# Low parts of the weights by an adding DMA, and tiles that begin on lines of 64 bytes

## The chip, the core and the metric

The kernel runs on one core of one Trainium2 chip. The metric is device microseconds of one launch. The engines are named as in the profile: PE (the tensor engine's matmuls), PEld (its weight loads), DVE (vector), ACT (scalar), POOL (gpsimd), SP (the engine that issues most DMAs); a transfer is carried out by the core's 16 DMA engines.

## The reference, cut to what matters

Two transformer-like blocks work one after the other on 512 tokens of 1024 features, in float32:

```python
def first_block(x, ...):
    for layer in range(2):
        if layer < 1: x = x + fox_mixer(rmsnorm(x, ...), w_fox_in, b_f, w_fox_out)   # 16 heads of 64
        else:         x = x + mla_mixer(rmsnorm(x, ...), w_dq, ..., w_mla_out, k, v) # 16 heads of 128 + 64
        x = x + conv_ffn(rmsnorm(x, ...), w_in, conv_w, conv_b, w_out)               # 1024 -> 2 x 2816 -> 1024
    return rmsnorm(x, final_norm)

def second_block(x, ...):
    x = x + nsa_pool_mixer(rmsnorm(x), ...)      # 8 heads, three branches, and a pooling branch
    x = x + swiglu(rmsnorm(x), ...)              # 1024 -> 2 x 2816 -> 1024
    x = x + conformer_conv(rmsnorm(x), ...)      # 1024 -> 2048, gate, 31-tap convolution, layer norm, -> 1024
    x = x + swiglu(rmsnorm(x), ...)
    return rmsnorm(x)
```

## The kernel before

Activations lie with the features on the 128 partitions and the 512 tokens along the row. A matrix product in nearly full float32 precision is made of three products in float32r, a rounded form that PE takes at full rate: each operand is a high part (rounded to float32r) and a low part (what the rounding left), and `mm3` (lines 320 to 323) adds high x high (L321), high weight x low activation (L322) and low weight x high activation (L323). A weight tile is 128 rows (partitions) by 1024 columns, 512 KB in float32: eight blocks of 128 x 128, so 24 matmuls with 512 moving columns each.

`load` (line 307) brings such a tile: a DMA issued by SP into `raw` (three buffers), a cast on ACT into `hi` (three buffers), and a subtraction on DVE into `lo` (three buffers), both in `split`, L303. It is called for all weights, 417 times. The other `split`s, of activations, stay as they are.

The stages follow each other: Fox attention, a gated FFN with a short convolution, MLA attention, the same FFN again, NSA attention, a SwiGLU FFN, the conformer, a SwiGLU FFN, the last norm. Each FFN is a loop over 44 tiles of its first matrix, with `xs` (`xsh` and `xsl`) as the moving operand, and then over eight output blocks of three loads each of its second matrix, with `hh` and `hl` as the moving operand. In the attention stages the heads run in a pipeline in which POOL scales the softmax (L522), and matmuls of projections fill PE's gaps. In the conformer the 31 taps of the convolution are shared by PE (with diagonal weights made by ACT, L1296, and DVE, L1297), DVE (L1269) and POOL (L1285, with products made by ACT, L1281).

The order of instructions on each engine is set when the program is built, by a scheduler that plays the program through with its own costs; loads get a higher priority. Each engine then runs its own list strictly in order and waits on semaphores.

Of the kernel before, what the change touches and what calls it, by code (L numbers as in the profile page):

```python
# [17 lines left out]
P = 128  # L18
T = 512
# [40 lines left out]
def _lay_out(i):  # L60
    """Only layout of the inputs, and constants of the shapes."""
# [147 lines left out]
class _Fill:  # L209
    """Tensor engine work that may stand between the steps of an attention, in order."""  # L210
# [7 lines left out]
    def push(self, name, gen, at=None, gate=None):  # L218
        """gate: (step of the heads, how many heads must be past it), for tiles that are used again."""
        self.q.insert(len(self.q) if at is None else at, (name, gen, gate))  # L220
# [22 lines left out]
    def need(self, name):  # L243
        """The task of this name, to its end."""
        for task in [t for t in self.q if t[0] == name]:
            self._all(task[1])
            self.q.remove(task)
# [7 lines left out]
def _body(ctx, tc, a, out):  # L255
# [14 lines left out]

    nvec = a["vecs"].shape[1]
    vecs = cp.tile([P, nvec], F32, name="vecs")
# [15 lines left out]
    gg = cp.tile([P, NC8], F32, name="gg")  # L288
    G.memset(ones, 1.0)
    mhalf = cp.tile([P, NQ], F32, name="mhalf")  # L290
# [9 lines left out]
    def split(hi, lo, src, scale=None):  # L300
        """hi + lo is src (times scale) to float32's precision; each is exact in float32r."""
        if scale is None:
            return S.copy(hi, src), V.tensor_sub(lo, src, bc(hi))  # L303
        return (S.activation(hi, src, AF.Copy, scale=scale),
                V.scalar_tensor_tensor(lo, src, scale, bc(hi), op0=OP.mult, op1=OP.subtract))  # L305

    def load(src, k, ahead=PRIO_DMA):
        n = src.shape[-1]
        with tc.high_priority(offset=ahead):
            raw = wp.tile([P, RAW], F32, tag="raw", name="raw", bufs=3)  # L310
            nc.sync.dma_start(raw[:, :n], src)
        with tc.high_priority(offset=min(ahead, PRIO_W)):
            hi = wp.tile([P, RAW], F32R, tag="hi", name="hi")
            lo = wp.tile([P, RAW], F32R, tag="lo", name="lo")
            split(hi[:, :n], lo[:, :n], raw[:, :n])
        return [z[:, :n].rearrange("p (k c) -> p k c", k=k) for z in (hi, lo)]
# [8 lines left out]
    def mm2(acc, w, rh, rl, first, last):  # L325
        """w: hi and lo beside each other, 64 columns each; their products are added by join()."""
        PE.matmul(acc, w, rh, start=first, stop=False)
        PE.matmul(acc, w, rl, start=False, stop=last)

    def join(hi, lo, po):  # L330
        S.copy(hi, po[:64])
        V.tensor_sub(lo, po[:64], bc(hi))
        V.tensor_add(lo, bc(lo), po[64:])
# [3 lines left out]
    def lin(acc, w, act, ks, cols, first=True, last=True, w0=0):  # L337
        """acc[cols, tokens] += sum over the chunks ks of w[k][:, cols].T @ act[k]."""
        wh, wl = w
        ah, al = act  # L340
        for n, k in enumerate(ks):
            mm3(acc, wh[:, k - w0, cols], wl[:, k - w0, cols], ah[:, k], al[:, k],
                first and n == 0, last and n == len(ks) - 1)
            yield STEP
# [8 lines left out]
    class Stats:  # L353
        """Sum over features of squares, gathered chunk by chunk."""
# [26 lines left out]
    def rsqrt(dst, src, n, eps):  # L381
        v = tp.tile([P, NQ], F32, name="var", tag="var", bufs=2)
        V.tensor_scalar(v, src, 1.0 / n, eps, op0=OP.mult, op1=OP.add)
        G.tensor_tensor(dst, v, mhalf, op=OP.pow)

    def wide(r):
        """[128 tokens, 4] -> the same for every partition, [128, 512]."""
        pr = bank("pr")
        for i in range(NQ):
            PE.transpose(pr[:, sl(i)], r[:, i : i + 1].to_broadcast([P, P]), ident)  # L390
        return pr
# [6 lines left out]
    class Norm:  # L398
        """Reciprocal root mean square of the tokens. What is made of it waits until the tensor
        engine has other work in hand: evictions that need it are put off by after()."""  # L400
# [7 lines left out]
        def step(self):  # L408
            if self.t is None:
                self.t = self.pool.tile([P, NQ], F32, name=self.name + "t", tag=self.name + "t", bufs=2)  # L410
                self.square(self.t)
            elif self.b is None:
                self.b = spread(self.t, self.pool, self.name)
                for f in self.put_off:
                    f()
                self.put_off = []
# [4 lines left out]
        def tick(self):  # L421
            """A tile of products has been queued."""
            self.left -= 1
            if self.left <= 0:
                self.step()
# [16 lines left out]
    def split_x(gname, dst=None, st=None, square_on=None):  # L442
        """x times its gain, as hi and lo."""
        dst = dst or xs
        for c in range(NC8):
            last = split(dst[0][:, c], dst[1][:, c], x[:, c], vec(gname, c))
            if st is not None:
                st.add(x[:, c], square_on)
        return last
# [9 lines left out]
    def out_proj(name, act, nk, per, blocks, b0=0, k0=0, late=False):  # L459
        """x += act @ weights; with late, the last chunk of act comes in after all others."""  # L460
# [20 lines left out]
    def stack_q(f, s, name, pool):  # L481
        """Head s of a pair: hi in its own half of the partitions, lo in the other half."""
        t = pool.tile([P, T], F32R, name=name, tag=name)
        S.copy(t[own[s]], f[own[s]])
        V.tensor_sub(t[own[1 - s]], f[own[s]], bc(t[own[s]]))
        return t

    def stack_k(f, s, ka, kl):
        """hi in both halves of ka, lo in the own half of kl."""
        S.copy(ka[own[s]], f[own[s]])  # L490
        V.tensor_copy(ka[own[1 - s]], f[own[s]])
        V.tensor_sub(kl[own[s]], f[own[s]], bc(ka[own[s]]))

    class Head:
        """Softmax attention of one head in three steps: scores, transposes, values."""
# [4 lines left out]
        def scores(self):  # L500
            pool = self.pool
            nm = pool.tile([P, NQ], F32, name="nm", tag="nm", bufs=3)
            sm = pool.tile([P, NQ], F32, name="sm", tag="sm", bufs=3)
# [10 lines left out]
            rc = pool.tile([P, NQ], F32, name="rc", tag="rc", bufs=3)  # L514
# [34 lines left out]
    def pipeline(prep, n, fill, edge):  # L549
        """Heads in a pipeline, with other work of the tensor engine between their steps."""  # L550
# [21 lines left out]
    # ------------------------------------------------------------------ Fox  # L572
    def fox():
        with ExitStack() as es:
# [27 lines left out]
            def forget():  # L602
# [4 lines left out]
                # softplus(z) with z = -logit: max(z, 0) + ln(1 + exp(-|z|))  # L607
# [83 lines left out]
    # ------------------------------------------------------------- gated FFN  # L691
# [44 lines left out]
    # ------------------------------------------------------------------ MLA  # L736
# [158 lines left out]
    # ------------------------------------------------------------------ NSA  # L895
    def nsa():
        with ExitStack() as es:
# [10 lines left out]
            ccmp = kp.tile([P, NQ * 32 + NQ], F32, name="ccmp")  # L908
# [9 lines left out]
            # two norms in a row: of x, and of what comes of it  # L918
# [8 lines left out]
            r1 = kp.tile([P, NQ], F32, name="r1")  # L927

            def square(t):
                rsqrt(r1, st1.sums(), D, EPS)  # L930
                m2 = tp.tile([P, NQ], F32, name="m2", tag="m2")
# [12 lines left out]
            with phase("n_x") as pool:  # L944
                # compressed keys and values
# [160 lines left out]
            # compressed branch  # L1106
# [82 lines left out]
    # ------------------------------------------------------------ conformer  # L1189
    def conformer():  # L1190
        with ExitStack() as es:
# [9 lines left out]
            with phase("c_x") as pool:  # L1201
# [3 lines left out]
                wdh = pool.tile([P, nw], F32R, name="wdh")  # L1205
                wdl = pool.tile([P, nw], F32, name="wdl")
# [3 lines left out]
                def conv(j, z, on, n_pe):  # L1210
                    """31 taps of chunk j: the first n_pe by the tensor engine, the rest by vector or gpsimd."""
                    y = zc[:, j]
                    if n_pe:
                        zh = pool.tile([P, T + 30], F32R, name="zh", tag="zh", bufs=2)
                        zl = pool.tile([P, T + 30], F32R, name="zl", tag="zl", bufs=2)
# [14 lines left out]
                # layer norm: sums about the mean of three chunks, and the exact shift from it  # L1230
# [88 lines left out]
                def beside(gen):  # L1319
                    """Tensor engine work, with the others' share of the convolutions beside it."""  # L1320
# [35 lines left out]
            rt = pool.tile([P, NQ], F32, name="lnt")  # L1356
            dt = pool.tile([P, NQ], F32, name="lndt")
            d2 = pool.tile([P, NQ], F32, name="lnd2")
# [30 lines left out]
    def final(gname):  # L1389
# [11 lines left out]
        rt = rp.tile([P, NQ], F32, name="rt", tag="rt", bufs=2)  # L1401
# [39 lines left out]
```

## Time and profile before

| what | value |
|---|---|
| median of 3 runs | 2606.76 us (2606.7 to 2606.8) |
| profiled execution, first to last instruction | 2603.5 us |
| the rest of a launch beside that span | about 3.3 us |
| PE busy | 2526.1 us, 97% |
| DVE busy | 1627.3 us, 63% |
| ACT busy | 1140.7 us, 44% |
| POOL busy | 464.8 us, 18% |
| DMA from HBM, mean | 84 GB/s; the one load queue takes 27.1% of 16 engines' time |

PE's busy share alone doesn't say that PE is the bound everywhere: it is a mean over stages, so the stretches below are read one by one.

### The profile page before, as it was taken

Reading aid. Unit: us, or ns where it says so; the run is one execution under the profiler, and the core shown is the slowest. Engines: PE = TensorE matmul, PEld = TensorE weight load, DVE = VectorE, ACT = ScalarE, POOL = GpSimd, SP = SyncE. Lnnn points to the kernel's source line nnn. Section 1 sums busy time; section 2 is a strip of 40 time slices with the busy share of each in tenths; the row PEclk is TensorE's granted clock in tenths of the full one; section 3 lists DMA queues with packets and bytes.
Section 4 is the critical chain, followed back from the end, with each engine's and each line's share of the span. In section 5 each row is a group of like instructions: output and inputs, shape, how many; then the busy total and the mean of one; then the engine's idle time right before and its main releaser. Section 6 shows DMA issues by size and latency. Waiting matters only on the chain. (4 is left out here: it accounts for less than half of the span.)

```text
span 2603.5 us, 31317 instructions
## 1 busy us (share of the span) xinstructions
PE 2526.1 (97%) x11903; PEld 2088.6 (80%) x11903; DVE 1627.3 (63%) x2495; ACT 1140.7 (44%) x1933; POOL 464.8 (18%) x369
## 2 busy tenths in 40 slices
PE   8999999999999999999999999999999778999998
PEld 6988888888888888888888888888887546888886
DVE  7887777625677656777436996444328996544422
ACT  4664444324566544444324684222225453333221
POOL 3452000001132212000011222000004763100001
PEclk9999999999999999999999999999999988999999
DMA  4122333333311222333333212333332101333332
GB/s 150 58 66 68 103 97 97 91 97 102 88 57 55 72 73 83 102 96 95 93 93 117 64 51 84 97 97 96 89 100 73 57 17 33 99 97 97 93 97 69
DMA packets 65447, 218.90 MB, mean 84 GB/s; under 512 B 7536, under 2 KB 8560, under 8 KB 65296
## 3 DMA queue, kind: packets, MB, share of 16 engines
q1 hardware_dynamic: 65296, 216.90, 27.1%
q8 instruction: 93, 1.52, 0.3%
q14 instruction: 58, 0.48, 0.1%
HBM read 214.70 MB, written 2.10 MB: 83 GB/s over the span
## 5 line engine op out<-in xcount | busy, mean ns | idle before, releaser
L303 ACT CAST hi<-raw 128x1024 fp32r<-128x1024 f32 (+4 forms) x417 | 420.5, 1010 | 919.5 <-PE acc L322 716.2
L323 PE MATMUL acc<-xsh,lo 128*128 128x512 f32 x1792 | 700.3, 391 | 15.7 <-DVE lo L303 15.7
L321 PE MATMUL acc<-xsh,hi 128*128 128x512 f32 x1792 | 699.6, 392 | 3.0 <-ACT xsh L303 2.9
L303 DVE TENSOR_TENSOR lo<-raw,hi 128x1024 fp32r<-128x1024 f32 (+4 forms) x417 | 499.8, 1199 | 322.8 <-ACT hi L303 317.7
L322 PE MATMUL acc<-xsl,hi 128*128 128x512 f32 x1792 | 700.5, 391 | 0.8 <-DVE xsl L305 0.8
L323 PEld LDWEIGHTS acc<-xsh,lo 128*128 128x128 f32 x1792 | 338.2, 189 | 88.9 <-DVE lo L303 18.7
L321 PEld LDWEIGHTS acc<-xsh,hi 128*128 128x128 f32 x1792 | 338.2, 189 | 73.6 <-ACT xsh L303 3.3
L322 PEld LDWEIGHTS acc<-xsl,hi 128*128 128x128 f32 x1792 | 338.0, 189 | 73.1 <-DVE xsl L305 2.1
L373 POOL TENSOR_TENSOR ssum<-ssum,sq 128x512 f32<-128x512 f32 x75 | 120.4, 1609 | 1482.3 <-ACT sq L367 1472.3
L321 PE MATMUL acc<-hh,hi 128*128 128x512 f32 x704 | 279.1, 396 | 0.0
L322 PE MATMUL acc<-hl,hi 128*128 128x512 f32 x704 | 279.1, 396 | 0.0
L323 PE MATMUL acc<-hh,lo 128*128 128x512 f32 x704 | 279.1, 396 | 0.0
L522 POOL TENSOR_SCALAR lg<-lg,rc 128x384 f32<-128x384 f32 (+3 forms) x144 | 165.8, 1167 | 384.2 <-DVE rc L515 300.6
L710 DVE TENSOR_TENSOR y<-acc,r 128x512 f32<-128x512 f32 x88 | 60.4, 691 | 219.7 <-PE acc L323 219.5
L457 DVE TENSOR_TENSOR x<-x,acc 128x512 f32<-128x512 f32 x104 | 70.6, 685 | 158.6 <-PE acc L323 158.3
L323 PEld LDWEIGHTS acc<-hh,lo 128*128 128x128 f32 x704 | 132.6, 188 | 32.3
L322 PEld LDWEIGHTS acc<-hl,hi 128*128 128x128 f32 x704 | 132.6, 188 | 32.3
L321 PEld LDWEIGHTS acc<-hh,hi 128*128 128x128 f32 x704 | 132.6, 188 | 32.3
L1285 POOL TENSOR_TENSOR zc<-zc,pr 128x496 f32<-128x496 f32 (+17 forms) x79 | 127.0, 1611 | 65.2 <-ACT pr L1281 56.7
L707 DVE SCALAR_TENSOR_TENSOR y<-u,vecs,y 128x510 f32<-128x510 f32 (+1 forms) x176 | 130.9, 748 | 3.4 <-ACT y L705 0.6
L512 ACT ACTIVATE lg<-lg,nm 128x128 f32<-128x128 f32 x192 | 107.1, 560 | 47.2 <-DVE nm L510 46.3
L303 ACT CAST hh<-y 128x512 fp32r<-128x512 f32 x88 | 54.6, 621 | 135.6 <-DVE y L714 135.6
(366 smaller groups left out, 3843.1 us busy)
## 6 DMA issues: line engine op xcount, KB each, us to landing
raw<-in_ffn_in SPq DMA_DIRECT2D x88, 512.0 KB
raw<-in_swi_in SPq DMA_DIRECT2D x88, 512.0 KB
raw<-in_ffn_out SPq DMA_DIRECT2D x32, 448.0 KB
raw<-in_swi_out SPq DMA_DIRECT2D x32, 448.0 KB
raw<-in_pw SPq DMA_DIRECT2D x24, 512.0 KB
raw<-in_fox_qk SPq DMA_DIRECT2D x16, 512.0 KB
raw<-in_ffn_out SPq DMA_DIRECT2D x16, 512.0 KB
raw<-in_uqk SPq DMA_DIRECT2D x16, 512.0 KB
```

What stands on the lines that cost most here:

```text
L303: return S.copy(hi, src), V.tensor_sub(lo, src, bc(hi))
L321: PE.matmul(acc, lh, rh, start=first, stop=False)
L322: PE.matmul(acc, lh, rl, start=False, stop=False)
L323: last_mm[0] = PE.matmul(acc, ll, rh, start=False, stop=last).ins
L373: (sum_on or G).tensor_add(self.s, self.s, sq)
L457: V.tensor_add(x[:, c], x[:, c], acc)
L512: S.activation(lg, lg, AF.Exp, bias=nm[:, i : i + 1], scale=-1.0, accum_out=sm[:, i : i + 1])
L522: (V if i in self.on_v else G).tensor_scalar(self.p[i], self.p[i], rc[:, i : i + 1], None, op0=OP.mult)
L707: V.scalar_tensor_tensor(y[:, sh:], u[:, : T - sh], vec(f"cw{l}{2 - sh}", jj), y[:, sh:], op0=OP.mult, op1=OP.add)
L710: V.tensor_mul(y, acc, norm.b)
L1285: G.tensor_add(y[:, sh:], y[:, sh:], pr[:, sh:])
```

## The change

`load` no longer uses DVE. ACT makes `hi` by a cast as before and then writes -1 times `raw`, rounded in the same way, into `lo`; POOL issues a DMA that reads the same weights a second time from HBM and adds them onto `lo`. What stands there then is weight minus rounded weight, as before. `raw` has two buffers in place of three, `lo` four in place of three. Each of the 417 loads so has one more DMA, on POOL's queue, which waits for ACT.

The second part is a helper `narrow`, which allocates a tile with its row rounded up to 16 floats, 64 bytes, and uses only the first columns. It is used for all tiles with rows of other lengths (`vecs`, the tiles of 4 columns such as `nm`, `sm`, `rc`, `var`, and some in the conformer). In the built program of before, `x`, `xs`, `raw`, `hi` and `lo` begin at multiples of 64 bytes in a partition, and `hh`, `hl`, `oh`, `ol`, `poh`, `pol`, `xkh`, `xkl`, `qlh`, `qll`, `lath`, `latl` and most operands of the heads 32 bytes past one. In the changed program every tile begins at a multiple of 64. The strings and comments that go change nothing.

```diff
+    def narrow(pool, n, dt=F32, **kw):
+
+        return pool.tile([P, -(-n // 16) * 16], dt, **kw)[:, :n]
+
     nvec = a["vecs"].shape[1]
-    vecs = cp.tile([P, nvec], F32, name="vecs")
+    vecs = narrow(cp, nvec, name="vecs")
...
-    mhalf = cp.tile([P, NQ], F32, name="mhalf")
+    mhalf = narrow(cp, NQ, name="mhalf")
...
     def load(src, k, ahead=PRIO_DMA):
         n = src.shape[-1]
         with tc.high_priority(offset=ahead):
-            raw = wp.tile([P, RAW], F32, tag="raw", name="raw", bufs=3)
+            raw = wp.tile([P, RAW], F32, tag="raw", name="raw", bufs=2)
             nc.sync.dma_start(raw[:, :n], src)
         with tc.high_priority(offset=min(ahead, PRIO_W)):
             hi = wp.tile([P, RAW], F32R, tag="hi", name="hi")
-            lo = wp.tile([P, RAW], F32R, tag="lo", name="lo")
-            split(hi[:, :n], lo[:, :n], raw[:, :n])
+            lo = wp.tile([P, RAW], F32R, tag="lo", name="lo", bufs=4)
+            S.copy(hi[:, :n], raw[:, :n])
+            S.mul(lo[:, :n], raw[:, :n], -1.0)
+
+            G.dma_start(lo[:, :n], src, accum_op=OP.add)
         return [z[:, :n].rearrange("p (k c) -> p k c", k=k) for z in (hi, lo)]
...
-            nm = pool.tile([P, NQ], F32, name="nm", tag="nm", bufs=3)
-            sm = pool.tile([P, NQ], F32, name="sm", tag="sm", bufs=3)
+            nm = narrow(pool, NQ, name="nm", tag="nm", bufs=3)
+            sm = narrow(pool, NQ, name="sm", tag="sm", bufs=3)
```

ACT's list in the first matrix of the first FFN, before. `hi` and `raw` are the weight tile's (the number tells tiles apart), `y0`, `u` and `hh` those of an output block's way to the second matrix:

```order
L303 CAST hi_3155<-raw_3153 128x1024
L713 ACTIVATE y0_2991<-y0_2991 128x512
L705 ACTIVATE y0_3069<-u_3070,vecs_70 128x512
L303 CAST hh_2864<-y0_2991 128x512
L303 CAST hi_3196<-raw_3194 128x1024
```

The same place in the changed program:

```order
L319 CAST hi_3397<-raw_3395 128x1024
L320 ACTIVATE lo_3436<-raw_3433 128x1024
L712 ACTIVATE y1_3305<-u_3306,vecs_70 128x512
L319 CAST hi_3435<-raw_3433 128x1024
L320 ACTIVATE lo_3478<-raw_3475 128x1024
```

The multiplication of a tile (`raw_3433`) stands a whole tile ahead of its cast: it is the first reader of `raw`, behind the cast of the tile before.

DVE's list in the conformer, before: taps of the convolution (`zc`) with the gate (`sg`, `z`) and the low part of one weight tile between them:

```order
L1330 TENSOR_TENSOR z_16732<-acc_16663,r_16612 128x512
L1269 SCALAR_TENSOR_TENSOR zc_16492<-z_16622,vecs_70,zc_16492 128x482
L1269 SCALAR_TENSOR_TENSOR zc_16492<-z_16622,vecs_70,zc_16492 128x483
L303 TENSOR_TENSOR lo_16802<-raw_16799,hi_16801 128x1024
L1269 SCALAR_TENSOR_TENSOR zc_16492<-z_16622,vecs_70,zc_16492 128x484
L1269 SCALAR_TENSOR_TENSOR zc_16492<-z_16622,vecs_70,zc_16492 128x485
L1269 SCALAR_TENSOR_TENSOR zc_16492<-z_16622,vecs_70,zc_16492 128x486
L1327 TENSOR_TENSOR sg_16729<-acc_16700,r_16612 128x512
```

And in the changed program:

```order
L1337 TENSOR_TENSOR z_17061<-acc_16991,r_16939 128x512
L1276 SCALAR_TENSOR_TENSOR zc_16817<-z_16949,vecs_70,zc_16817 128x482
L1276 SCALAR_TENSOR_TENSOR zc_16817<-z_16949,vecs_70,zc_16817 128x483
L1276 SCALAR_TENSOR_TENSOR zc_16817<-z_16949,vecs_70,zc_16817 128x484
L1276 SCALAR_TENSOR_TENSOR zc_16817<-z_16949,vecs_70,zc_16817 128x485
L1276 SCALAR_TENSOR_TENSOR zc_16817<-z_16949,vecs_70,zc_16817 128x486
L1334 TENSOR_TENSOR sg_17058<-acc_17029,r_16939 128x512
```

The weight tile's subtraction is gone from between the taps; the rest keeps its order.

POOL's list in the conformer, before, at its own taps (`pr` are products that ACT made):

```order
L384 TENSOR_TENSOR rt_16572<-var_16578,mhalf_79 128x4
L1285 TENSOR_TENSOR zc_16492<-zc_16492,pr_16763 128x482
L1285 TENSOR_TENSOR zc_16492<-zc_16492,pr_16768 128x483
L1285 TENSOR_TENSOR zc_16492<-zc_16492,pr_16777 128x484
L1285 TENSOR_TENSOR zc_16492<-zc_16492,pr_16786 128x485
```

And in the changed program:

```order
L322 DMA lo_17238<-in_pw1 128x1024
L1292 TENSOR_TENSOR zc_16817<-zc_16817,pr_17093 128x482
L1292 TENSOR_TENSOR zc_16817<-zc_16817,pr_17098 128x483
L1292 TENSOR_TENSOR zc_16817<-zc_16817,pr_17107 128x484
L322 DMA lo_17292<-in_pw1 128x1024
L1292 TENSOR_TENSOR zc_16817<-zc_16817,pr_17116 128x485
```

The adding DMAs of the weights of the first pointwise matrix (`in_pw1`) stand between the taps, one after every third.

## Rows read from the trace of the kernel before

**Rows 1.** The page: PE's busy time, and its tenths in 40 slices.

```profile
PE 2526.1 (97%) x11903; PEld 2088.6 (80%) x11903; DVE 1627.3 (63%) x2495; ACT 1140.7 (44%) x1933; POOL 464.8 (18%) x369
...
PE   8999999999999999999999999999999778999998
```

**Rows 2.** Stretches of 65 us: Fox, first and second FFN matrix, NSA, conformer twice.

```profile
core 0: us, PE busy (x) PEld busy (x) DVE busy (x) ACT busy (x) POOL busy (x), PEclk, DMA share, GB/s
130.00:195.00 65.00, 65.00 (x398) 58.31 (x397) 55.62 (x129) 42.51 (x103) 32.97 (x28) 1.00 0.21 66
390.00:455.00 65.00, 65.00 (x288) 53.83 (x287) 47.44 (x61) 29.08 (x37) 0.00 (x0) 1.00 0.31 98
520.00:585.00 65.00, 65.00 (x279) 52.28 (x278) 19.67 (x21) 16.75 (x20) 6.21 (x4) 1.00 0.33 95
1495.00:1560.00 65.00, 62.32 (x355) 52.33 (x355) 60.89 (x186) 57.53 (x158) 18.50 (x17) 0.97 0.19 57
2015.00:2080.00 65.00, 50.95 (x198) 39.45 (x196) 65.00 (x55) 32.48 (x48) 48.55 (x30) 0.93 0.18 57
2080.00:2145.00 65.00, 44.40 (x144) 30.14 (x144) 64.97 (x90) 36.00 (x84) 43.31 (x30) 0.84 0.05 17
```

**Rows 3.** Chain of waits, conformer: shares by line, then start, us, what.

```profile
by line: DVE zc L1269 44.8%; DVE dl L1297 19.3%; DVE lo L303 11.3%; issue 7.1%; DVE z L1331 4.8%; DVE zl L303 2.7%; DVE zc L1264 2.3%; DVE d L1237 2.0%; DVE ssum L373 2.0%; DVE z L1330 1.8%; DVE sg L1327 1.2%; DVE zc L1313 0.4%; DVE s L1254
...
1996.26 2.18 DVE lo L303
...
2034.53 1.13 DVE lo L303
```

**Rows 4.** PE's timeline, MLA: start us, us, line, operation, tiles.

```profile
649.58 0.39 PE L321 MATMUL acc<-xsh,hi 128*128 128x512 f32 x1
...
655.01 0.40 PE L321 MATMUL acc<-xkh,hi 128*128 128x512 f32 x1
...
660.38 0.40 PE L323 MATMUL acc<-xkh,lo 128*128 128x512 f32 x1
```

**Rows 5.** Groups by line and shape: count, busy us, mean ns, idle before.

```profile
L303 DVE TENSOR_TENSOR lo<-raw,hi 128x1024 fp32r<-128x1024 f32 x328 | 411.0, 1254 | 209.6 <-ACT hi L303 206.5
L303 ACT CAST hi<-raw 128x1024 fp32r<-128x1024 f32 x328 | 343.9, 1051 | 649.0 <-PE acc L322 470.0 <-issue 121.6 <-PE pq L322 18.4
...
L321 PE MATMUL acc<-hh,hi 128*128 128x512 f32 x704 | 279.1, 396 | 0.0
...
L321 PE MATMUL pq<-qlh,hi 128*128 128x512 f32 x144 | 58.3, 405 | 0.0
...
L321 PE MATMUL acc<-oh,hi 128*128 128x512 f32 x96 | 38.0, 401 | 0.2 <-DVE nm L510 0.2
...
L321 PE MATMUL acc<-poh,hi 128*128 128x512 f32 x32 | 13.1, 410 | 0.3 <-DVE ol L333 0.2
...
L321 PE MATMUL pq<-lath,hi 128*128 128x512 f32 x32 | 13.1, 408 | 0.0
```

**Rows 6.** The instructions that read tile xkh: durations, starts, forms.

```profile
L321 PE MATMUL acc<-xkh,hi x24: 395/396/478, 655.0 to 672.4; 128*128 128x512 f32 x16, 128*64 128x512 f32 x8
```

**Rows 7.** Two stretches, instructions on tile lo alone: PE, PEld, DVE.

```profile
130.00:195.00 65.00, 28.91 (x85) 16.27 (x86) 9.86 (x9) 1.00 0.21 66
1495.00:1560.00 65.00, 10.87 (x27) 5.07 (x27) 5.17 (x5) 0.97 0.19 57
```

**Rows 8.** POOL's timeline in the conformer, columns as in rows 4.

```profile
1985.68 17.15 POOL L1285 TENSOR_TENSOR zc<-zc,pr 128x482 f32<-128x482 f32 x10 [20.03 <-ACT pr L1281]
...
2035.40 4.75 POOL L1285 TENSOR_TENSOR zc<-zc,pr 128x506 f32<-128x506 f32 x3 [3.94 <-ACT pr L1281]
```

**Rows 9.** Timeline of the start, all engines.

```profile
1.18 0.42 SPq L280 DMA_DIRECT2D x<-in_xt  x1
...
4.16 0.69 DVE L369 TENSOR_TENSOR ssum<-x 128x512 f32<-128x512 f32 x1 [4.16 <-DMA x<-in_xt]
...
7.53 0.28 DVE L303 TENSOR_TENSOR lo<-raw,hi 128x128 fp32r<-128x128 f32 x1
```

More of the change, by code (lines that the diff above doesn't have):

```diff
@@ L287, in _body @@
     ones = cp.tile([P, P], F32, name="ones")
-    gg = cp.tile([P, NC8], F32, name="gg")
+    gg = narrow(cp, NC8, name="gg")
     G.memset(ones, 1.0)
-    mhalf = cp.tile([P, NQ], F32, name="mhalf")
+    mhalf = narrow(cp, NQ, name="mhalf")
     G.memset(mhalf, -0.5)
@@ L381, in rsqrt @@
     def rsqrt(dst, src, n, eps):
-        v = tp.tile([P, NQ], F32, name="var", tag="var", bufs=2)
+        v = narrow(tp, NQ, name="var", tag="var", bufs=2)
         V.tensor_scalar(v, src, 1.0 / n, eps, op0=OP.mult, op1=OP.add)
@@ L409, in step @@
             if self.t is None:
-                self.t = self.pool.tile([P, NQ], F32, name=self.name + "t", tag=self.name + "t", bufs=2)
+                self.t = narrow(self.pool, NQ, name=self.name + "t", tag=self.name + "t", bufs=2)
                 self.square(self.t)
@@ L513, in scores @@
                 self.p.append(lg)
-            rc = pool.tile([P, NQ], F32, name="rc", tag="rc", bufs=3)
+            rc = narrow(pool, NQ, name="rc", tag="rc", bufs=3)
             V.reciprocal(rc, sm)
@@ L907, in nsa @@
             gates = kp.tile([P, NQ, 24], F32, name="gates")
-            ccmp = kp.tile([P, NQ * 32 + NQ], F32, name="ccmp")
+            ccmp = narrow(kp, NQ * 32 + NQ, name="ccmp")
             nc.sync.dma_start(ccmp, a["c_cmp"])
@@ L926, in nsa @@
             norm = Norm(st1, D, rp, "r", NT_N)
-            r1 = kp.tile([P, NQ], F32, name="r1")
+            r1 = narrow(kp, NQ, name="r1")
             def square(t):
                 rsqrt(r1, st1.sums(), D, EPS)
-                m2 = tp.tile([P, NQ], F32, name="m2", tag="m2")
+                m2 = narrow(tp, NQ, name="m2", tag="m2")
                 V.tensor_mul(m2, st2.sums(), r1)
@@ L1204, in conformer @@
                 wdw = vecs[:, _VECS["w_dw"][0] : _VECS["w_dw"][0] + nw]
-                wdh = pool.tile([P, nw], F32R, name="wdh")
-                wdl = pool.tile([P, nw], F32, name="wdl")
+                wdh = narrow(pool, nw, F32R, name="wdh")
+                wdl = narrow(pool, nw, name="wdl")
                 S.copy(wdh, wdw)
@@ L1213, in conv @@
                     if n_pe:
-                        zh = pool.tile([P, T + 30], F32R, name="zh", tag="zh", bufs=2)
-                        zl = pool.tile([P, T + 30], F32R, name="zl", tag="zl", bufs=2)
+                        zh = narrow(pool, T + 30, F32R, name="zh", tag="zh", bufs=2)
+                        zl = narrow(pool, T + 30, F32R, name="zl", tag="zl", bufs=2)
                         for t in (zh, zl):
@@ L1355, in conformer @@
             pool = es.enter_context(phase("c_y"))
-            rt = pool.tile([P, NQ], F32, name="lnt")
-            dt = pool.tile([P, NQ], F32, name="lndt")
-            d2 = pool.tile([P, NQ], F32, name="lnd2")
+            rt = narrow(pool, NQ, name="lnt")
+            dt = narrow(pool, NQ, name="lndt")
+            d2 = narrow(pool, NQ, name="lnd2")
             pd = bank("pd")
@@ L1400, in final @@
             PE.matmul(pt[:, i : i + 1], sq[:, sl(i)], ones[:, 0:1], start=False, stop=True)
-        rt = rp.tile([P, NQ], F32, name="rt", tag="rt", bufs=2)
+        rt = narrow(rp, NQ, name="rt", tag="rt", bufs=2)
         rsqrt(rt, pt[:, :NQ], D, EPS)
```

## Prediction

> **What bounds the kernel now.** The page comes first [rows 1]: the tensor engine (PE) is busy in 2526.1 of the 2603.5 us of the span, and the slices show where it is not: at the start, around slices 32 to 34, and at the end. Then the table of stretches [rows 2], six pieces of 65 us from the kinds of work that matter. In the gated FFNs PE is busy in all 65.00 us at a granted clock of 1.00, while the vector engine (DVE) is busy in 47.44, the scalar engine (ACT) in 29.08, the gpsimd engine (POOL) in none, and the DMA engines in 0.31 of the time. So there the split of the weights on DVE is already hidden, and taking it away gains nothing. In the conformer the picture is turned round: DVE is busy in 65.00 and 64.97 of 65 us, PE in 50.95 and 44.40, and the granted clock is down to 0.93 and 0.84 on the mean: after PE's gaps it spends part of the time at the lower of its two levels, 1.2 instead of 2.4 GHz. Last the chain of waits of that stretch [rows 3]: from 1981 to 2168 us it runs on DVE, and 11.3% of it is `lo`, the very operation that goes.
>
> PE has a second property that matters here: its matmuls of 512 columns don't all take the same time. In the first FFN matrix 288 start in 65 us, 225.7 ns each; in the second 279, 233.0 ns each [rows 2]. PE waits for nothing in either.
>
> **The change part by part: where tiles begin.** The moving operand of the first FFN matrix (`xs`) begins at a multiple of 64 bytes, that of the second (`hh`, `hl`) 32 bytes past one. Is that the cause? The MLA stage has both operands back to back [rows 4]. Up to 655.01 us PE reads `xs`: 24 matmuls from 649.58, 226.3 ns each. From 655.01 it reads `xk`, which begins 32 bytes past: 23 steps to 660.38, 233.5 ns each, with the same kind of weight and nothing else changed. So the step is 7.2 ns there and 7.3 in the FFNs; I take 6.8, since a few of the 279 are slowed by other things. After the change every tile begins at a multiple of 64. The 512-column matmuls that now read a shifted operand are 704 + 144 + 96 + 32 + 32 [rows 5] and 24 [rows 6], in each of the three products: 1032 x 3 = 3096. That is 3096 x 6.8 ns = 21 us, all of it where PE is the bound. The score matmuls of the heads have shifted operands too; they are narrower, some 280 of 512 columns' worth by the loops of the kernel, another 2 us. Together -23 us (bounds: 0, if the cause is another, and -25).
> The Trainium skill (SBUF — State Buffer, "Specifications (TRN2)") puts SBUF's lines at 16 bytes, by which a tile 32 bytes in begins on a line as well as any other and this term would be 0. The trace speaks against it, with 226.3 beside 233.5 ns, but what it shows is a coincidence of operand and offset, so the rule is kept as a rival below.
>
> **What leaves DVE.** 417 subtractions, 328 of them of 1254 ns [rows 5]. In the FFNs and attention stages PE is busy throughout [rows 2], so they are worth nothing there. In the conformer they are worth what stands on the chain: 11.3% of 187 us, 21 us [rows 3]. One `lo` there lasts 2.18 us where POOL works beside it (at 1996.26) and 1.13 where POOL is idle (at 2034.53) [rows 3, 8]. What is late next is the rest of the same DVE work, the taps (L1269) and the diagonals (L1297), which keep the chain, so most of the 21 us should come off. But POOL, with 48.55 of 65 us busy on its own taps, now also issues a DMA every three taps there, and ACT takes the multiplications. I take -15 us (bounds: 0, and -40 if PE's clock no longer falls in the 130 us of the two stretches).
>
> **What ACT gets.** 417 multiplications by -1 of the shape of the `hi` cast, 1051 ns for 1024 columns [rows 5]; with a scalar a row of this size may take a sixth more. In an FFN stretch of 12 weight tiles (288 / 24) that is 12 x 1.05 = 12.6 us on 29.08: 41.7 of 65, hidden by PE. In Fox nine `lo` are made in the stretch and in NSA five [rows 7]: 42.51 + 9 x 1.05 = 52 us, hidden, and 57.53 + 5 x 1.05 = 62.8, barely. The order of ACT does one thing well: the multiplication of the next tile stands ahead of that tile's `hi` cast, and as `lo` has four buffers and `hi` three, both wait for the same release by PE. So the add starts some 2 us after PE has left tile t-3 and is needed when PE comes to t+1: three tiles of 5.42 us, 16.3 us, less 2.1 on ACT, leaves 14 us. A load of 256 KB at the start took 2.98 us from issue to its first reader (1.18 to 4.16, [rows 9]). Even several times that is covered. The raw load has two buffers in place of three; its slot comes free when the cast is done, about 4.4 us before ACT wants the next, and a late one stalls only ACT, which has 23 us to spare in 65.
>
> **What the DMA engines get.** This is the term that decides. 417 transfers read the weights a second time, and each also reads and writes `lo` in SBUF. The raw loads take 0.31 x 65 / 12 = 1.68 us of all 16 engines for a tile of 512 KB [rows 2]. An adding transfer is nowhere in this trace. From below it costs as much as a plain one, 1.68 us; from above, if its two reads and its write follow each other without overlap, three times that, 5.04. I take two streams, 3.36 us, because a plain load already has one read and one write in its 1.68, and only the read is added. Then a tile asks for 1.68 + 3.36 = 5.04 of 5.42 us: 93% full, but under it, with 14 us of cover for queueing. It stays hidden up to 3.74 us (5.42 - 1.68), and above that the FFNs run at the pace of the DMA engines. POOL, which issues them, is idle in the FFNs [rows 2].
> The Trainium skill (Collectives: The Full Stack, "The bandwidth ceiling: the fold count and why AG ≠ RS ≠ AR") says that a DMA that adds is slower because it reads two sources and not because of the adding, and gives a measured ratio of 1.93. As an estimate from that page the add would take 3.24 us and the tile 4.92; no row here shows an adding transfer.
>
> **The start.** The first `lo` is a subtraction of 0.28 us at 7.53 [rows 9], and PE takes it at once. Now a multiplication, an issue and a transfer of about 3 us stand there, while 3.5 MB of other loads are under way; PE has first products to do meanwhile. +4 us (bounds 0 and +8).
>
> **Sum.** -23 - 15 + 4 = -34 us on the profiled execution, 2603.5 us of span and about 3.3 around it, 2606.8 together, which is also the median of the runs. 2606.8 - 34 = 2573 us.
>
> **Rivals.**
> First, the adding transfer is too slow: the DMA engines become the bound of the FFNs. For it: the margin is only 0.38 us in 5.42 and nothing here has measured it. Against: a share of 0.31 now, and 14 us of cover. At three passes a tile takes 6.72 us, 1.30 more than PE needs. The four FFNs load 44 tiles of 512 KB each and 22 tiles' worth in the second matrix, 264 in all: 264 x 1.30 = 343 us, and the 14 us of aligned second matrices (2112 x 6.8 ns) don't show: 2573 + 14 + 343 = 2930. It decides from 3.74 us on; each 0.1 us over that costs 26 us. Chance 0.19.
> Second, ACT and POOL become what DVE was in NSA and the conformer. For it: ACT at 57.53 of 65 in NSA, POOL at 48.55 in the conformer, both in order, and POOL's issue waits for ACT's multiplication with the softmax scaling or the taps queued behind it, for which PE or the layer norm waits. Against: both have idle time in every stretch shown. If the 51 weight tiles of these two stages (27 and 24 by their loads) each put their multiplication on the path, 51 x 1.05 = 54 us, and DVE's 15 us aren't won: 2606.8 - 23 + 4 + 54 = 2642. It decides when ACT's sum in a stretch reaches the 65 us. Chance 0.09.
> Third, the change of the tiles doesn't do what it seems to: where a tile begins is not what costs 6.8 ns. Then 2606.8 - 15 + 4 = 2596. Chance 0.10.
>
> **How the numbers follow.** Forecast 0.61, the rivals 0.19, 0.09 and 0.10, and 0.01 for what I haven't thought of. The forecast's own range is 2552 to 2594 (the conformer's -40 with the full alignment, or nothing from the conformer with a late start). The whole range takes in the third and the second rival and a slightly slow add: 2548 to 2660; it leaves out most of the first rival. A change of 0.2%, 5 us, is about what a measurement of this kernel can tell from none. Faster: nearly all of the forecast and most of the third rival, 0.68. Slower: the first and second rivals and a little of the rest, 0.26. The same: 0.06.
>
> **What would show it.** In the table of stretches: second FFN matrices at 288 matmuls in 65 us as the first (alignment); the DMA share in the FFNs near 0.9 with PE still at 65 of 65 (the add at two streams), or PE below it and the share near 1 (first rival). In the chain of waits: the conformer's DVE stretch near 165 us without `lo`. In PE's waits: none for POOL's transfers but at the start. The prediction is wrong if `lo` by DMA stands among PE's longest waits.

## The result, and the profile after

The changed kernel takes 2622.4 us (2618.7 to 2626.7, four runs) beside 2606.8 (2606.7 to 2608.6) for the kernel before: 1.006 times as long, with a 95% interval of 1.0045 to 1.0074. It is slower by 0.6%, where 2573 us and a gain had been forecast. The profiled execution spans 2623.2 us beside 2603.5, so 19.7 us are to be found.

In this case the FFNs are landmarks. In both profiles the 528 recorded matmuls of every second matrix are timed from the first to the last, and the 1056 of a first matrix take 240.6 us in both wherever PE doesn't wait at its start. With each FFN's start counted back from there, the rest falls to the other stages (what PE waits for in the first tiles of an FFN is counted to the stage ahead of it). "Lines" is the first experiment below, tiles on 64-byte lines without the adding DMA:

| us, profiled execution | before | lines | after |
|---|---|---|---|
| start and Fox | 256.6 | 256.4 | 264.6 |
| second FFN matrix, each of four | 123.5 | 120.6 | 120.6 |
| MLA | 387.4 | 383.8 | 383.2 |
| NSA | 220.6 | 222.1 | 245.0 |
| conformer | 267.1 | 267.0 | 268.5 |
| last norm | 15.6 | 14.9 | 17.0 |
| span | 2603.5 | 2589.2 | 2623.2 |

Each column is one profiled execution, and the one of the changed kernel, 2625.0 us as a launch, lies 2.6 us above that kernel's median; so a difference of two or three us in one stage is not safe.

The lines bring 14.3 us. The adding DMA costs 34.0, of them 22.9 in NSA and 8.2 at the start, and in the conformer it brings nothing. Stretches of the kernel after, with columns as in [rows 2]:

```profile
130.00:195.00 65.00, 64.86 (x424) 58.74 (x423) 49.78 (x128) 48.85 (x113) 36.00 (x34) 1.00 0.50 111
390.00:455.00 65.00, 65.00 (x288) 53.81 (x288) 34.37 (x48) 39.06 (x48) 10.39 (x12) 1.00 0.87 194
520.00:585.00 65.00, 65.00 (x286) 53.33 (x285) 7.20 (x10) 29.95 (x36) 16.24 (x17) 1.00 0.92 193
...
1400.00:1430.00 30.00, 22.27 (x153) 19.12 (x152) 12.50 (x19) 21.25 (x29) 5.30 (x7) 0.85 0.88 206
1430.00:1460.00 30.00, 30.00 (x139) 25.07 (x139) 17.86 (x37) 14.77 (x27) 4.33 (x5) 0.87 0.78 184
...
1495.00:1560.00 65.00, 59.55 (x348) 50.60 (x346) 55.77 (x182) 57.76 (x162) 19.79 (x20) 0.97 0.30 71
...
0.00:20.00 20.00, 8.21 (x20) 2.77 (x20) 13.69 (x13) 11.76 (x16) 13.71 (x21) 1.00 0.86 267
20.00:40.00 20.00, 17.09 (x95) 13.95 (x96) 4.62 (x6) 6.03 (x6) 7.57 (x7) 1.00 0.91 193
```

Two stretches answer to the FFN rows of [rows 2]: PE is still busy in 65.00 of 65, the second matrix has 286 matmuls in place of 279, and the DMA share has gone from 0.31 and 0.33 to 0.87 and 0.92. So in the FFNs the add is hidden, as forecast. The rows from 0 to 40 us and from 1400 to 1460 us are of places whose DMA share the prediction did not read. The same places before:

```profile
0.00:20.00 20.00, 11.93 (x39) 6.55 (x40) 13.84 (x15) 8.86 (x12) 11.57 (x17) 1.00 0.81 275
20.00:40.00 20.00, 19.84 (x136) 17.09 (x134) 13.28 (x17) 6.31 (x9) 5.78 (x4) 1.00 0.32 106
1400.00:1430.00 30.00, 29.83 (x201) 24.72 (x201) 26.25 (x35) 19.13 (x30) 0.11 (x1) 1.00 0.46 145
1430.00:1460.00 30.00, 30.00 (x166) 26.18 (x165) 25.64 (x54) 9.43 (x18) 1.73 (x2) 0.94 0.19 57
```

The share was already 0.81 in the first 20 us and 0.46 early in NSA, where PE was idle for only 0.2 of the 30 us. After, PE is idle for 7.7 of these 30 us and the granted clock falls to 0.85: PE's gap is followed by time at 1.2 GHz in place of 2.4. PE's longest waits in NSA and the first tiles of the next FFN (us in total, times, longest):

```profile
PE ph L329 <- DMA lo<-in_cw: 7.7, 2, 3.9
PE acc L330 <- DMA lo<-in_swi_in: 3.7, 1, 3.7
PE sc L1164 <- DVE nm L517: 2.0, 2, 1.7
```

`in_cw` are the weights of NSA's compression. Their products have 128 moving columns, not 512:

```profile
1412.61 0.37 PE L329 MATMUL ph<-lo,bh 128*64 128x128 f32 x1 [3.91 <-DMA lo<-in_cw]
...
1413.20 0.31 PE L328 MATMUL ph<-hi,bh 128*64 128x128 f32 x1
1413.31 0.31 PE L329 MATMUL ph<-lo,bh 128*64 128x128 f32 x1
```

One starts every 0.11 us here, behind the gap and at the lower clock, so PE is done with such a tile of 512 KB in 24 x 0.11 = 2.6 us, in place of 5.42 in the FFNs. In the kernel before, at a granted clock of 1.00, the 48 matmuls of two tiles follow each other without a gap:

```profile
1408.89 0.22 PE L321 MATMUL ph<-hi,bh 128*64 128x128 f32 x1
...
1411.76 0.44 PE L321 MATMUL pq<-xsh,hi 128*128 128x512 f32 x1
```

That is 2.87 us for two, 1.4 us a tile. The two waits for transfers, 7.7 and 3.7 us, are 11.4 of the 22.9 us; that the lower clock behind them (0.87 from 1430 to 1460 us, 0.94 before) makes up most of the rest is likely, but the profile does not divide it.

What the transfers need is seen in an FFN stretch of 12 tiles (share of 16 engines over 65 us; the last line has the median from issue to landing):

```profile
q0 software_dynamic: 1722, 6.27, 57.3%
q1 hardware_dynamic: 1732, 6.31, 29.3%
...
lo<-in_ffn_in POOLq DMA_DIRECT2D x12, 512.0 KB, 6.4
```

The adding queue (q0) takes 0.573 x 65 / 12 = 3.10 us of 16 engines for a tile and the plain one 1.59.

### The profile page after: what moved, and what is told of

Its sections match the earlier page's. It is cut to its first block, busy times and chain, and to the rows that moved or that the text cites. A ratio compares the mean times of both kernels' runs of the same rounds, so it can differ in the third digit from the quotient of the medians.

```text
span 2623.2 us, 32062 instructions
## 1 busy us (share of the span) xinstructions
PE 2519.1 (96%) x11903; PEld 2095.6 (80%) x11903; DVE 1169.8 (45%) x2078; ACT 1499.7 (57%) x2350; POOL 785.6 (30%) x786
## 4 chain that ended last, share of the span: by engine, by line
PE 86%; DVE 8%; DMA 2%; ACT 1%; issue 1%; POOL 1%; SPq 0%; DVEq 0%; POOLq 0%; ACTq 0%
PE acc L328 22%; PE acc L330 22%; PE acc L329 22%; DVE zc L1276 4%; PE pq L328 3%; PE pq L330 3%; PE pq L329 2%; PE pt L537 2%; DVE dl L1304 1%; PE pv L328 1%; PE pv L329 1%; PE pv L330 1%; PE po L335 1%; PE po L334 1%; POOL zc L1292 1%
## 5 line engine op out<-in xcount | busy, mean ns | idle before, releaser
L320 ACT ACTIVATE lo<-raw 128x1024 fp32r<-128x1024 f32 (+4 forms) x417 | 423.3, 1015 | 99.8 <-DMA raw<-in_swi_in 26.7
L329 PE MATMUL acc<-hl,hi 128*128 128x512 f32 x704 | 273.2, 388 | 0.0
L529 POOL TENSOR_SCALAR lg<-lg,rc 128x384 f32<-128x384 f32 (+3 forms) x144 | 157.7, 1106 | 140.5 <-DVE rc L522 81.6
L322 POOL DMA_DIRECT2D lo<-in_swi_in x88 | 76.2, 865 | 384.4 <-ACT lo L320 373.8
L717 DVE TENSOR_TENSOR y<-acc,r 128x512 f32<-128x512 f32 x88 | 60.4, 691 | 290.5 <-PE acc L330 266.7
L322 POOL DMA_DIRECT2D lo<-in_ffn_in x88 | 76.2, 866 | 375.9 <-ACT lo L320 364.8
L1292 POOL TENSOR_TENSOR zc<-zc,pr 128x496 f32<-128x496 f32 (+16 forms) x79 | 122.4, 1563 | 32.4 <-ACT pr L1288 24.6
```

The costliest lines, as they stand in the source:

```text
L320: S.mul(lo[:, :n], raw[:, :n], -1.0)
L322: G.dma_start(lo[:, :n], src, accum_op=OP.add)
L329: PE.matmul(acc, lh, rl, start=False, stop=False)
L529: (V if i in self.on_v else G).tensor_scalar(self.p[i], self.p[i], rc[:, i : i + 1], None, op0=OP.mult)
L1292: G.tensor_add(y[:, sh:], y[:, sh:], pr[:, sh:])
```

## The experiments

Each was timed in the same session as the kernel before; ratios are to it. "Sub" is DVE's subtraction, "add" the changed way.

**Lines alone**: `load` as before, `narrow` kept.

```diff
...
-            S.copy(hi[:, :n], raw[:, :n])
-            S.mul(lo[:, :n], raw[:, :n], -1.0)
-
-            G.dma_start(lo[:, :n], src, accum_op=OP.add)
+            split(hi[:, :n], lo[:, :n], raw[:, :n])
```

> Only the tiles on 64-byte lines; the low parts of the weights by DVE as before. Measured with both parts, 528 matmuls of a second FFN matrix take 120.6 us instead of 123.5, so 4 x 2.8 = 11 us in the FFNs, and some 7 us in the attention stages: 2606.8 - 18 = 2589 us (2586 to 2592) if the lines alone do this. If the shorter matmuls came from the other part of the change, the time stays within 3 us of 2606.8.

2592.6 us, 0.9941 (0.9928 to 0.9953). The lines alone shorten the second FFN matrices, all by the same 2.9 us, and MLA by 3.6; in the attention stages less came than I had put down for this run, and the time is just above its range.

**The add alone**: `narrow` without its rounding.

```diff
-        return pool.tile([P, -(-n // 16) * 16], dt, **kw)[:, :n]
+        return pool.tile([P, n], dt, **kw)
```

> Only the adding DMA, tiles where they began before. If the two parts add up: 2622.4 + 14 (the lines alone were worth 2606.4 - 2592.6) = 2636 us, with 123.5 us for a second FFN matrix and 245, 265 and 268 us for NSA, the start with Fox, and the conformer as in the changed kernel. If the lines are worth something only without the adds, or the adds hide part of them: 2625 or less.

2637.6 us, 1.0119 (1.0105 to 1.0133), as expected: the parts add up. NSA took 238.9 us, the start with Fox 268.6 and the conformer 268.3, so single stages shift by some us either way while the whole fits.

**A copy in place of the add**, **no second DMA**, and **three raw and three lo buffers**:

```diff
-            G.dma_start(lo[:, :n], src, accum_op=OP.add)
+            G.dma_start(lo[:, :n], src.bitcast(F32R))
```
```diff
-            G.dma_start(lo[:, :n], src, accum_op=OP.add)
```
```diff
-            raw = wp.tile([P, RAW], F32, tag="raw", name="raw", bufs=2)
+            raw = wp.tile([P, RAW], F32, tag="raw", name="raw", bufs=3)
-            lo = wp.tile([P, RAW], F32R, tag="lo", name="lo", bufs=4)
+            lo = wp.tile([P, RAW], F32R, tag="lo", name="lo", bufs=3)
```

> The changed kernel, but POOL's second DMA copies the weights over lo instead of adding them (lo then holds the weights, not their low parts). POOL's list, its waits and ACT's multiplications stay; only the reading of lo goes from the transfers. Theory A (where weight tiles are wanted fast, at the start and at NSA's compression weights, the DMA engines can't bring both transfers; in the conformer POOL's in-order list holds back its taps): the DMA share in the FFNs falls from 0.88 to about 0.6, NSA (after ffn1 to the first matmul of the next FFN) regains 5 to 10 of its lost 24 us, the conformer stays as it is; 2605 to 2612 us. Rival B (two raw buffers instead of three make loads late) and rival C (the 417 multiplications on ACT's in-order list): nothing comes back but 1 or 2 us, 2618 to 2624.

> The changed kernel without the second DMA (lo holds the negated weights, not their low parts). ACT's multiplications, two raw buffers and the lines stay, POOL issues no DMA. Theory A: start and NSA are as short as before or shorter, and the conformer shows the 15 us that were forecast, since DVE has no subtraction and POOL's taps wait for no transfer: 2589 - 15 = 2574 us (2566 to 2582). Rivals B and C: start and NSA stay as slow as in the changed kernel, 2600 to 2620.

> The changed kernel with three raw and three lo buffers instead of two and four. Rival B: the losses at the start, in NSA and at the next FFN go, 2589 to 2600 us. Theory A: no better than the changed kernel, 2618 or more, since the transfers and POOL's list stay as they are and lo has a tile less of lead (an add then has 16.3 - 5.4 - 2.1 = 9 us, with 6.7 from issue to landing). Rival C: 2622.

| us | start, Fox | NSA | conformer | median | ratio to before |
|---|---|---|---|---|---|
| changed kernel | 264.6 | 245.0 | 268.5 | 2622.4 | 1.0060 |
| a copy | 266.7 | 231.8 | 261.1 | 2605.5 | 0.9994 (0.9985 to 1.0003) |
| no second DMA | 255.7 | 226.0 | 254.0 | 2582.0 | 0.9905 (0.9892 to 0.9919) |
| three raw, three lo | 275.0 | 250.2 | 279.7 | 2668.1 | 1.0238 (1.0222 to 1.0254) |

Without the second DMA, ACT's multiplications and the two raw buffers are still there, and the loss is gone: rivals B and C fall as main causes. They keep at most 3.9 us in NSA (226.0 beside 222.1 with lines alone). A third raw buffer at the price of a lo buffer makes all worse, so the lead of `lo` counts; what a third raw buffer is worth by itself, this run can't say. (A first matrix took 245 to 257 us there, beside 241 to 247 before, and what it lost is counted to the stage ahead of it.) Of PE's list of waits there:

```profile
PE acc L330 <- DMA lo<-in_pw: 18.5, 7, 5.2
...
PE pq L330 <- DMA lo<-in_nsa_q: 6.5, 2, 4.6
...
PE acc L330 <- DMA lo<-in_ffn_in: 5.9, 2, 3.8
```

The copy gives back 13.2 us in NSA, more than expected, 7.4 in the conformer, which had been expected to stay as it is, and nothing at the start: there, a second transfer of either kind costs 9 to 11 us. Its queue in the same FFN stretch as above:

```profile
q0 software_dynamic: 1728, 6.29, 33.6%
q1 hardware_dynamic: 1718, 6.25, 29.2%
...
lo<-in_ffn_in POOLq DMA_DIRECT2D x12, 512.0 KB, 4.4
```

That is 1.82 us of 16 engines for a tile and 4.4 from issue to landing, beside 3.10 and 6.4 for the add.

**Sub in Fox and for the four `in_cw` tiles**, add elsewhere:

```diff
+            if vector or how[0] == "sub":
+                split(hi[:, :n], lo[:, :n], raw[:, :n])
...
-                        w1 = load(a["cw1"][m * 2 + half], 8)
+                        w1 = load(a["cw1"][m * 2 + half], 8, vector=True)
...
+    how[0] = "sub"
     fox()
+    how[0] = "add"
     conv_ffn(0)
```

> The changed kernel with DVE's subtraction, without a second DMA, in Fox and for the four tiles of NSA's compression weights; the adding DMA for all other loads. Theory A (the loss lies where many bytes are wanted in a short time): Fox takes 256 us instead of 265, NSA 233 instead of 245 (7.7 us of waiting for these tiles, and some 4 that PE then spends at the lower clock), FFNs as now: 2622.4 - 8 - 12 = 2602 us. If the wait only moves on to the next tiles (NSA's q, k and u weights), NSA stays at 240 or more: 2612 us.

2612.3 us, 1.0022 (1.0012 to 1.0031). Fox is back at 257.9 us, but NSA takes 240.8: the wait moves on, as the second alternative had it. PE's waits in NSA and the next FFN's first tiles:

```profile
PE pq L334 <- DMA lo<-in_nsa_q: 9.3, 2, 6.7
PE acc L334 <- DMA lo<-in_swi_in: 3.5, 2, 3.1
```

**Add in the conformer alone**, lines everywhere, sub elsewhere (two raw and four lo buffers kept):

```diff
...
+    how[0] = "add"
     conformer()
+    how[0] = "sub"
     swiglu(1)
```

> Lines everywhere; the adding DMA in the conformer alone (16 tiles of the first pointwise matrix and 8 of the second), DVE's subtraction elsewhere. Theory A (POOL's own list with 17 issues in it is what eats DVE's gain): the conformer takes 268 us as in the changed kernel and not 254 as without the DMA; DVE's taps end at some 165 us into it and POOL's at 206; 2592.6 + 1.5 = 2594 us (2590 to 2599). Rival D (the conformer is late because of what comes before, adds in the FFN on either side that fill the DMA engines): it takes some 255 us, 2580 us.

2594.5 us, 0.9953 (0.9939 to 0.9966), and 267.2 us for the conformer: its lost gain is its own affair. Where it goes is read from POOL. In the changed kernel, lines of POOL's work there (busy us, mean ns, idle before it), then its longest wait:

```profile
L1292 POOL TENSOR_TENSOR zc<-zc,pr 128x496 f32<-128x496 f32 (+16 forms) x79 | 122.4, 1563 | 32.4 <-ACT pr L1288 24.6 <-DVE dl L1304 4.0
L322 POOL DMA_DIRECT2D lo<-in_pw x17 | 15.2, 892 | 35.6 <-ACT lo L320 35.6
...
POOL lo L322 <- ACT lo L320: 35.6, 10, 6.6
```

The same without the second DMA:

```profile
L1291 POOL TENSOR_TENSOR zc<-zc,pr 128x496 f32<-128x496 f32 (+17 forms) x79 | 121.3, 1539 | 62.9 <-ACT pr L1287 58.7
```

And POOL's timeline in the changed kernel, where a tap stands behind an issue that waits:

```profile
2049.55 6.55 POOL L1292 TENSOR_TENSOR zc<-zc,pr 128x500 f32<-128x500 f32 x4
2060.12 0.88 POOL L322 DMA_DIRECT2D lo<-in_pw  x1 [4.02 <-ACT lo L320]
2060.73 4.92 POOL L1292 TENSOR_TENSOR zc<-zc,pr 128x504 f32<-128x504 f32 x3
```

The taps themselves cost the same (122.4 and 121.3 us). What is new in POOL's list is 15.2 us of issuing and 35.6 of waiting for ACT's multiplications with taps queued behind; 30.5 us less of idle time before the taps pays for part of it. Counted from the end of the FFN before, DVE's taps end at 165 us in place of 206, but POOL's at 206 in place of 201, and without the DMA at 192. Over most of the stage (1995 to 2200 us) the chain of waits is still DVE's, with POOL at 6.6% of it (first line; without the DMA, from 1960 to 2160 us, POOL is not among its larger shares, second line):

```profile
by line: DVE zc L1276 47.2%; DVE dl L1304 13.4%; POOL zc L1292 6.6%; DVE zc L1271 3.7%; DVE z L1338 2.9%; PE acc L328 2.8%; PE acc L329 2.7%; PE acc L330 2.4%; issue 1.8%; DVE z L1337 1.8%; DVE sg L1334 1.8%; DVE d L1244 1.7%; DVE zl L307 1
...
by line: DVE zc L1275 49.6%; DVE dl L1303 18.1%; DVE z L1337 4.0%; PE acc L327 3.7%; PE acc L328 3.4%; PE acc L329 3.2%; DVE ssum L379 2.4%; DVE zc L1270 2.1%; DVE d L1243 2.1%; DVE z L1336 1.8%; DVE sg L1333 1.8%; issue 1.4%; PE pd L1367 0
```

It is the end, 2167 to 2184 us, that runs over POOL, and there DVE waits 7.17 us for it (shares by line; then start, us, what of the chain; then DVE's timeline):

```profile
by line: POOL zc L1292 79.9%; issue 8.4%; DVE zc L1271 4.1%; DVE d L1244 4.1%; DVE ssum L380 3.9%; ACT pr L1288 3.6%; POOLq L1292 0.9%
...
2181.26 1.27 POOL zc L1292
...
2182.55 0.69 DVE L1271 TENSOR_TENSOR zc<-zc,cmean 128x512 f32<-128x512 f32 x1 [7.17 <-POOL zc L1292]
```

With the copy, POOL's 17 issues take less, and the conformer 261.1 us:

```profile
L322 POOL DMA_DIRECT2D lo<-in_pw x17 | 9.6, 564 | 36.3 <-ACT lo L320 36.2
```

**Fewer taps on POOL**: PE takes 20, then 26 taps of chunk 4 in place of 12, with the add in the conformer alone; and 20 with lines alone as the control.

```diff
-CONV_ON = [..., (4, "g", 12), ...]
+CONV_ON = [..., (4, "g", 20), ...]
```

> As the kernel with the adding DMA in the conformer alone, and there PE takes 20 taps of chunk 4 instead of 12, so POOL has 71 taps instead of 79. Theory A (POOL's list is the conformer's bound once DVE has no subtractions): 8 taps of 1.55 us leave it, its last tap ends 12 us sooner, DVE gets 8 diagonals of 0.6 us and PE 8 x 0.7 us, both with time to spare: the conformer takes 258 us (254 to 262) instead of 268, and the whole 2594 - 10 = 2584 us. If POOL's list isn't the bound, the conformer stays at 266 or more, 2592 us or more.

> The adding DMA in the conformer alone, and PE takes 26 taps of chunk 4, POOL 65. At 20 taps POOL's last tap ended at 189 us and DVE's sums at 200, so POOL is no longer last there: 6 more diagonals of 0.63 us on DVE make it 2 to 4 us longer, 2586 + 3 = 2589 us; if POOL still counted, 6 x 1.6 us would go, 2578 us.

> The kernel with lines alone (DVE's subtraction everywhere), and PE takes 20 taps of chunk 4 instead of 12, POOL 71 instead of 79. Theory A: with the subtractions DVE is the bound of the conformer; POOL's relief is worth nothing and DVE gets 8 more diagonals of 0.6 us: 267 to 273 us for the conformer, 2592 to 2598 us. If the 8.7 us that the same shift gave beside the adding DMA came from the shift alone, the conformer takes 258 us, 2584 us.

| | conformer, us | POOL's last tap | median | ratio to before |
|---|---|---|---|---|
| add in the conformer, 12 taps | 267.2 | 204.5 | 2594.5 | 0.9953 |
| the same, 20 taps | 258.5 | 188.7 | 2586.0 | 0.9925 (0.9911 to 0.9938) |
| the same, 26 taps | 259.5 | 175.4 | 2588.3 | 0.9930 (0.9917 to 0.9944) |
| lines alone, 12 taps | 267.0 | 201.3 | 2592.6 | 0.9941 |
| lines alone, 20 taps | 262.4 | 176.4 | 2583.9 | 0.9915 (0.9900 to 0.9930) |

POOL was last with 12 taps and no longer is with 20, as expected. The control missed: in the conformer half of the gain (4.6 of 8.7 us) comes without any add, and by the ratios of the whole kernels nearly all of it (0.26 of 0.28%, with an interval of about 0.13% either way on each). So the shift of taps does not show that all of the 8.7 us were POOL's. DVE's diagonals show where the control's gain comes from, in the same stretch from 2122 to 2160 us of the two kernels with lines alone (12 taps, then 20; count, busy us, mean ns):

```profile
L1301 DVE TENSOR_SCALAR dl<-ident,wdl 128x128 fp32r<-128x128 f32 x26 | 14.6, 589 | 0.0
```
```profile
L1301 DVE TENSOR_SCALAR dl<-ident,wdl 128x128 fp32r<-128x128 f32 x30 | 7.4, 279 | 0.0
```

With 12 taps POOL is at its own until 2147 us, with 20 it has done them by 2120. The mean of 589 ns hides two kinds, which the timelines of the first kernel show (POOL, then DVE):

```profile
2133.10 1.82 POOL L1289 TENSOR_TENSOR zc<-zc,pr 128x506 f32<-128x506 f32 x1 [9.30 <-ACT pr L1285]
...
2142.34 5.00 POOL L1289 TENSOR_TENSOR zc<-zc,pr 128x510 f32<-128x510 f32 x3 [2.59 <-ACT pr L1285]
...
2126.14 0.28 DVE L1301 TENSOR_SCALAR dl<-ident,wdl 128x128 fp32r<-128x128 f32 x1
...
2144.23 1.31 DVE L1301 TENSOR_SCALAR dl<-ident,wdl 128x128 fp32r<-128x128 f32 x1
```

A diagonal in POOL's pause of 9.30 us takes 0.28 us, one beside POOL's taps up to 1.31. POOL slows DVE, as the 2.18 and 1.13 us of a `lo` in [rows 3, 8] had shown. Lines alone with 20 taps is the fastest of the versions that leave nothing out, 22 us below the kernel before; the add with 20 taps lies within its interval.

**Lo buffers of its own for the conformer** (eight, for the first pointwise matrix), three of raw, hi and lo elsewhere, 20 taps:

```diff
...
+                lo = own.tile([P, RAW], F32R, tag="wlo", name="lo", bufs=8)
```

> Lines everywhere; buffers as before (three of raw, hi and lo) and DVE's subtraction for all loads but those of the conformer's first pointwise matrix: these get eight lo buffers of their own and the adding DMA; PE takes 20 taps of chunk 4. Against the kernel with PE at 20 taps and two raw, four lo buffers (2586.0): Fox, MLA and the tail win back the 1.4 + 1.5 + 0.6 us that two raw buffers cost there beside DVE's subtraction; in the conformer, if what POOL waits for (35 us behind ACT's multiplications) came from lo buffers that PE still held, it gets shorter by 5 or more, 2577 us; if it came from ACT's in-order list, it stays at 258, 2583 us.

2593.4 us, 0.9951 (0.9939 to 0.9964): both alternatives missed. The conformer takes 270.8 us, and PE waits 11.5 us for the first add. ACT's first multiplications of that stage, here (the FFN ahead ends at 1944.2 us) and with the common buffers (it ends at 1948.4):

```profile
1945.30 2.95 ACT L324 ACTIVATE lo<-raw 128x1024 fp32r<-128x1024 f32 x3
```
```profile
1935.10 1.04 ACT L325 ACTIVATE lo<-raw 128x1024 fp32r<-128x1024 f32 x1
```

Here three come at once, 1.1 us after the FFN; with the common buffers the first is 13.3 us ahead of its end. The new buffers are tiles of the conformer's own phase, which takes over the FFN's memory, and that is the likely reason. Whether deeper buffers would free POOL this run does not say.

## Why the prediction was wrong, step by step

The direction failed at two steps, and one term was too large. The sign named for being wrong came true: the adding DMAs of `in_cw` head PE's waits in NSA, with 7.7 us. That 2622.4 us lies in the whole range of 2548 to 2660 us is luck: it was drawn that wide for the rivals and a slightly slow add, and the time came from NSA's transfers.

*The cover of the adding transfer.* "14 us of cover" and "93% full" were worked out for the FFNs and taken to hold for every stage but the start. In the FFNs they are right: PE is busy in 65.00 of 65 us. For NSA only ACT's sum was worked out ("busy throughout" was a misreading of PE's 62.32 of 65 us in [rows 2]), and the step of taking the FFN's tile as the measure failed there: at a granted clock of 1.00 PE goes through a compression tile in 1.4 us, and the profile of before had a DMA share of 0.46 in that stretch. With 3.10 / 1.59 = 1.95 more for the add, that asks, as an estimate, for 0.46 x 2.95 = 1.36 of the engines. Measured: +22.9 us, of which the no-DMA run leaves 3.9, a second plain transfer with its issue on POOL adds 5.8 and the adding another 13.2. The second rival's mechanism (PE late for softmax scaling behind an issue on POOL) is not seen in NSA: none of PE's waits there names POOL. Sparing the `in_cw` tiles alone gave back 4.2 us, since the next tiles are late then. Whether in NSA the engines' share or the length of a tile's chain (load, multiplication, issue, 6 to 9 us to landing) ends the wait isn't separated; the share was 0.88, not 1, while PE waited.

*The conformer's gain.* DVE is relieved as forecast, and without the DMA the conformer takes 254.0 us, 13 less than with lines alone: the -15 were right for DVE alone. With the add, POOL's taps end last, at 206 us with DVE waiting for them, and the conformer is 1.5 us longer than with lines alone. That is the mechanism of the second rival (an issue that waits for ACT with the taps queued behind it), which had 9%; its price of 54 us was too high. The run with 20 taps on PE bears it out only in part, since half of its gain comes without the add. In the forecast POOL's 48.55 of 65 us busy were read as room, though its list is in order.

*The lines.* Right in kind: the third rival falls with the first experiment. But -23 was -14.3. A second matrix went from 123.5 to 120.6 us, 2.9 / 528 = 5.4 ns a matmul instead of 6.8. One on `hl` is now followed by the next after 226 ns, as on `xs`, one on `hh` after 229 to 232; why is open. The rest of the difference lies in the attention stages, where NSA was 1.5 us longer with lines alone.
The Trainium skill (SBUF — State Buffer, "Specifications (TRN2)") speaks of lines of 16 bytes; with lines alone the 32 bytes cost 2.9 us in every second matrix, so the measurement decides against taking this as all that counts for a matmul's operand.

*The price of the add.* 3.36 us were taken, 3.10 measured, under the 3.74 from which the FFNs would have slowed: the first rival did not come true, with about 0.7 us of 5.42 to spare (1.59 + 3.10 = 4.69).
The Trainium skill (Collectives: The Full Stack, "The bandwidth ceiling: the fold count and why AG ≠ RS ≠ AR") has a measured ratio of 1.93 between two collectives, one whose DMAs copy and one whose DMAs add; the traces agree for single transfers, with 1.95 beside the plain loads; beside a copy on the same queue it is 1.70 (57.3% beside 33.6%).

*The start.* +4 with bounds 0 and +8; it was +8.2. Its reason was the one `lo` that PE waits for, and that wait is 1.8 us in PE's list; more lies elsewhere, likely in the other loads, which come later with the share at 0.86 and 0.91 (PE waits 2.9 us for a later `hi` that it did not wait for before).

*ACT* stayed hidden in Fox, with 48.85 us busy in the stretch for the 52 forecast, and in NSA, with 57.76 for 62.8 (but for the 3.9 us at most). The multiplication took 1056 ns beside the cast's 1049, not a sixth more.

*The range.* The forecast's own range does not follow from its bounds: 2552 puts the late start's +8 beside the -40 (without it the end is 2544), and -23 with nothing from the conformer and a late start is 2592, not 2594. Nothing here turns on it.

So of -23 - 15 + 4 = -34 came -14.3 + 1.5 + 8.2, and NSA's +22.9, MLA's -0.6 and the last norm's +2.1, which had no term: +19.8 us for 19.7 seen.

## What to carry to other kernels

A transfer hidden by a steady loop is not hidden by the kernel: look for the stretches in which the share is already highest, and for tiles that are used by narrow matmuls, and work the sum there. Before work is moved off the engine that bounds a stage, write out the in-order list of the engine that gets the issue, with what that issue waits for; idle time in it is not free where its next work is queued behind the wait. And take a change of several parts apart: here one half was worth 0.6% and the other cost 1.2%.

## What the runs showed of the hardware

- An adding DMA took 3.10 us of 16 engines for 512 KB, beside 1.59 for a plain load and 1.82 for a copy from POOL's queue; 6.4 us from issue to landing, and 4.4 for the copy.
- Its issue kept POOL busy for 0.89 us in the conformer, that of a copy 0.56.
- FFN stretches ran at full pace with the DMA engines at 0.87 to 0.92, as long as `lo` had four buffers; with three, a second matrix took up to 121.6 us in place of 120.6.
- DVE's 128 x 128 multiplications took up to 1.31 us beside POOL's taps and 0.28 in POOL's pauses: 589 ns on the mean in a stretch with both, and 279 where POOL was done.
- Matmuls of 128 moving columns started every 0.06 us at a granted clock of 1.00 and every 0.11 us behind a gap, at 1.2 GHz.
